# Feed-forward output projections as eight Strassen groups and three plain groups

## The chip, the cores and the metric

The kernel runs on one core of one Trainium2 chip. The metric is the device time of one execution in microseconds. PE is the matrix engine (TensorE), DVE the vector engine, ACT the scalar engine, POOL GpSimd, SP the engine that issues most transfers.

## The reference, cut to what matters

Two transformer blocks work on 512 rows of 1024 numbers in float32. Between them they hold three feed-forwards of the same sizes (1024 to twice 2816, and 2816 back to 1024), each followed by a norm:

```python
def _conv_ffn(x, w_in, conv_w, conv_b, w_out):        # twice, in the first block
    u = x @ w_in
    u = sum(conv_w[j] * up[:, j:j + s] for j in range(CONV_WIDTH)) + conv_b
    g, val = u[..., :D_FF], u[..., D_FF:]
    return (jax.nn.silu(g) * val) @ w_out
...
x = _layer_norm(DN_ALPHA * x + f, ln_ffn_g[layer], ln_ffn_b[layer])
...
gate, up = jnp.split(h2 @ w_gate_up[i], 2, axis=-1)   # once, in the second block
ffn = (jax.nn.silu(gate) * up) @ w_down[i]
x = x + rms_norm(ffn, norm2_post[i])
```

## The kernel before, in words

Every number is carried as a high and a low part in the engine's reduced float32 format, and a product takes three matmuls: high by high, high by low, low by high. `split` (L189) makes the parts: ACT copies the high part, DVE subtracts it to get the low part. `wchunk` (L172) loads 1024 columns of weights into one of three raw buffers and splits them into one of four `whi`/`wlo` buffers.

The 2816 inner columns are worked in 11 groups of 256. For a group, `w_in(g)` loads four weight chunks (two of the gate, two of the value), and `ws_pairs` (L221) runs 96 matmuls of 512 columns into PSUM: gate and value of the first 128 columns, then of the second 128, 24 matmuls each. They use a pool of three PSUM banks named `mm`; a second pool of four is named `at`. The weight buffers of a group come free one by one in its second half, when the next group's chunks are split into them.

In the first two feed-forwards (`ffn`, L829, called `ffn0` and `ffn1` below) each PSUM bank then passes a convolution of three taps (L836 on ACT, L838 twice on DVE), the gate a Silu (L843), and the product of gate and value (L845) is split into `hh`/`hl`. After six groups the output projection of the first 11 blocks of 128 runs (`out_proj`, L610, through `xs`, L240), after the other five that of the last 11. A block of 128 costs 24 matmuls of 512 columns: four row tiles, two column halves, three matmuls (L257 to L259). The result is added to `self.x` by `res_epi` (L383) with the residual scaled by ALPHA in the first half. In the last half `xs` holds back the last four chunks (`stagger=4`), so that each row tile ends by itself and its layer norm and its transposes (`need`, `later`) run beside the matmuls of the next tile; the last column half sits in the `mm` banks.

In the third feed-forward (`ffn2`, L1486) the output projection of ten of the groups goes by Strassen's scheme in Winograd's form, two groups to a phase (`st_phase`, L1422). `st_operands` (L1392) makes seven 256-wide blocks of a group's inner columns with four DVE sums, and splits them. A phase forms four sums of weight blocks on DVE (L1457 to L1462), splits seven weight blocks, and runs seven products of 12 matmuls (L1439 to L1441). Each product fills two PSUM banks, which ACT copies (first phase) or DVE adds (L1447) into one of seven accumulators. In the last phase the accumulators are summed between the products (L1453). Group 11 is plain, with both column halves of a row tile in one go (`xsn`, L626, matmuls L637 to L639), and the RMS norm of each row tile follows it (L1523 to L1532); the residual tile `x2` is loaded from memory on ACT's queue into one of two buffers.

The order on each engine is made by a scheduler at build time that moves independent instructions past each other; each engine then runs its list in order.

Of the kernel before, what the change touches and what calls it, by code (L numbers as in the profile page):

```python
# [15 lines left out]
S = 512  # L16
D = 1024
# [63 lines left out]
class K:  # L81
# [747 lines left out]
    def ffn(self, l, pool, post, hook):  # L829
        nc, I = self.nc, self.I  # L830
        W1, W2 = I["ffn_w_in"][l], I["ffn_w_out"][l]
        hT = {}
# [8 lines left out]
        def pair(m, gp, vp):  # L841
            g = conv(gp, m)
            nc.scalar.activation(g, g, AF.Silu)  # L843
            v = conv(vp, KF + m)
            nc.vector.tensor_tensor(out=v, in0=g, in1=v, op=ALU.mult)  # L845
            hT[m] = (pool.tile([P, S], F32R, tag="hh", name="hh", bufs=12), pool.tile([P, S], F32R, tag="hl", name="hl", bufs=12))
            self.split(v, *hT[m])

        def w_in(g):
            gc = self.ws_load(W1, g * 256)  # L850
            vc = self.ws_load(W1, DFF + g * 256)
            for mm_, gp, vp in self.ws_pairs(gc, vc, g == 0):
                pair(g * 2 + mm_, gp, vp)

        def w_out(k0, kt, last):
            self.out_proj(W2, k0, kt, lambda k: hT[k0 + k][0], lambda k: hT[k0 + k][1], 1.0 if last else ALPHA, post if last else None)

        for g in range(6):
            w_in(g)
            if g == 1:  # L860
                hook()
        w_out(0, 11, False)
        for g in range(6, 11):
            w_in(g)
        w_out(11, 11, True)
# [555 lines left out]

    def st_phase(self, pool, B, hs, Q, first, bufs, last=False):  # L1422

# [4 lines left out]
        b11, b12, b21, b22 = B[0, 0], B[0, 1], B[1, 0], B[1, 1]  # L1428

        def product(i, block, raw, bank):  # L1430
            w = self.wsplit(raw)
            ps = [bank(), bank()]
            for p in range(2):
                h, l = hs[p]
                for t in range(2):
                    a = h[:, block * 256 + t * P:block * 256 + (t + 1) * P]
                    b = l[:, block * 256 + t * P:block * 256 + (t + 1) * P]
                    wh, wl = (x[:, p * 512:(p + 1) * 512] for x in w)
# [3 lines left out]
            for t in range(2):  # L1442
                q = Q[i][:, t * 512:(t + 1) * 512]
                if first:
                    nc.scalar.activation(q, ps[t], AF.Copy)
                else:
                    V(out=q, in0=ps[t], in1=q, op=ALU.add)  # L1447

        def sum_(a, b, op=ALU.add):
            if last:  # L1450
                for t in range(2):
                    s = slice(t * 512, (t + 1) * 512)
                    V(out=Q[a][:, s], in0=Q[a][:, s], in1=Q[b][:, s], op=op)  # L1453

        t2 = pool.tile([P, 1024], F32, tag="wr", name="wr", bufs=bufs)
        product(0, 0, b11, self.psa)
# [3 lines left out]
        product(6, 5, b12, self.psa)  # L1460
        product(5, 4, t2, self.psum)
        V(out=t2, in0=t2, in1=b21, op=ALU.subtract)  # L1462
        sum_(5, 0)
        sum_(6, 5)
        product(1, 1, b21, self.psa)
        sum_(0, 1)
        product(4, 3, b11, self.psa)
        sum_(5, 4)
        sum_(4, 6)
        sum_(6, 3, ALU.subtract)  # L1470
        product(2, 6, b22, self.psum)
        sum_(5, 2)
        if last:
            Q[3] = Q[6]
            V = lambda out, in0, in1, op: nc.vector.tensor_tensor(out=out, in0=in1, in1=in0, op=ALU.subtract)
        product(3, 2, t2, self.psa)
# [9 lines left out]
    def ffn2(self, pool):  # L1486
# [3 lines left out]
        acc = pool.tile([P, 7, D], F32, name="acc")  # L1490
        Q = {i: acc[:, i, :] for i in range(7)}
        xd = self.xd.rearrange("(t p) d -> t p d", p=P)
        hs, B = {}, {}
        WR = 6

        def w_in(g):
# [7 lines left out]
            if g < 10:  # L1504
                return lambda: hs.setdefault(g, self.st_operands(pool, R))
            else:
                hs[g] = [pool.tile([P, self.BLOCKS], F32R, tag=n, name=n, bufs=3)[:, :1024] for n in ("hh", "hl")]
                self.split(R[:, :1024], *hs[g])

        sst = [self.sm.tile([P, 2], F32, tag="ss3", name="ss3") for _ in range(NT)]  # L1510

        def blk(t, c):
            return Q[((0, 5), (6, 4))[t // 2][c]][:, t % 2 * 512:(t % 2 + 1) * 512]

        def last(c):
            sl = slice(c * 512, (c + 1) * 512)

            def epi(t, ps):
                if c == 0:
                    xt[t] = pool.tile([P, D], F32, tag="x2", name="x2", bufs=2)  # L1520
                    nc.scalar.dma_start(xt[t], xd[t])
                a = blk(t, c)
# [4 lines left out]
                if c == 1:  # L1527
                    r = self.rstd2(sst[t])
                    for i in range(2):
                        s = slice(i * 512, (i + 1) * 512)  # L1530
                        nc.vector.scalar_tensor_tensor(out=xt[t][:, s], in0=blk(t, i), scalar=r, in1=xt[t][:, s], op0=ALU.mult, op1=ALU.add)
# [3 lines left out]
        xt = {}  # L1535
        w_in(0)()
        w_in(1)()
        for g in range(0, 10, 2):
            B = self.st_load(pool, W2, g, WR)
            rest = w_in(g + 2)  # L1540
            self.st_phase(pool, B, (hs[g], hs[g + 1]), Q, g == 0, WR, g == 8)
            if g < 8:
                rest()
                w_in(g + 3)()
        h, l = hs[10]
        self.xsn([(W2, c * 512, last(c)) for c in range(2)], 2, lambda k: h[:, k * 512:(k + 1) * 512], lambda k: l[:, k * 512:(k + 1) * 512], 20)

    def run(self):
# [4 lines left out]
        with tc.tile_pool(name="xp", bufs=1) as xp:  # L1553
# [8 lines left out]
            with tc.tile_pool(name="ffn0", bufs=1) as pool:  # L1562
                G, B = self.bcast(I["ln_ffn_g"][0], "G", pool), self.bcast(I["ln_ffn_b"][0], "B", pool)
                dpool = tc.tile_pool(name="diffc", bufs=1, side="right")
                dp = dpool.__enter__()
                self.ffn(0, pool, self.norm_post(G, B, pool.tile([P, S], F32, name="jk")), lambda: self.load1(dp))
# [3 lines left out]
            with tc.tile_pool(name="ffn1", bufs=1) as pool:  # L1570
                G, B = self.bcast(I["ln_ffn_g"][1], "G", pool), self.bcast(I["ln_ffn_b"][1], "B", pool)
                G1 = self.bcast(I["norm1_pre_2"][0], "G1", pool)
# [3 lines left out]
                jk = pool.tile([P, S], F32, name="jk")  # L1576

                def post(t):
                    self.layer_norm(t, G, B, jk)
                    nc.gpsimd.dma_start(xd[t], self.x[:, t, :])  # L1580
                    h = pool.tile([P, D], F32, tag="hn", name="hn", bufs=4)
                    ss = self.sm.tile([P, 2], F32, tag="ss4", name="ss4")
                    for i in range(2):
                        hs = slice(i * 512, (i + 1) * 512)
                        nc.scalar.activation(jk, self.x[:, t, hs], AF.Square, scale=1.0 / 32, accum_out=ss[:, i:i + 1])
                    r = self.rstd2(ss)
                    for i in range(2):
                        hs = slice(i * 512, (i + 1) * 512)
                        nc.vector.scalar_tensor_tensor(out=h[:, hs], in0=self.x[:, t, hs], scalar=r, in1=G1[:, hs], op0=ALU.mult, op1=ALU.mult)
                    self.later(t, lambda: self.to_T(h, t))  # L1590
                self.ffn(1, pool, post, lambda: self.load2(self.kp))
# [30 lines left out]
```

## Time and profile before

| | |
|---|---|
| median of 3 runs | 2115.29 us (2115.05 to 2115.59) |
| the profiled execution | 2115.29 us, its span 2113.1 us |
| PE busy in the span | 2057.3 us (97%) |
| DVE busy | 1416.6 us (67%) |
| ACT busy | 1045.1 us (49%) |
| mean granted PE clock | 0.995 |

The span is the time from the first to the last instruction, so about 2 us of the execution lie outside it. Busy is the union of an engine's instructions; a matmul's own duration overlaps the next one's, so its cost is read from the distance of two starts. In the rows, `A<-B` is what an instruction writes and reads, and the part in brackets or after the last bar is how long the engine sat idle before it and what released it.

### The profile page before, as it was taken

To read this page: it belongs to the slowest core of one execution; us is meant where nothing else is said; L and a number is where in the kernel's file an instruction comes from. 1 tells how busy PE (TensorE), PEld (TensorE's weight loads), DVE (VectorE), ACT (ScalarE), POOL (GpSimd) and SP (SyncE) were. 2 spreads that over 40 slices of the span, in tenths; PEclk is the share of its full clock that TensorE was granted. 3 is DMA by queue.
4 is the path that set the end of the run, shared out by engine and by line. 5 is a ranking of instruction groups with operands and counts; after the bars stand their busy time and mean duration, and the time that the engine had idled before them with its cause. 6 is when DMAs were issued, how large, how long until landed. Compare 5 with 4: busy or idle time off the path is not lost.

```text
span 2113.1 us, 28021 instructions
## 1 busy us (share of the span) xinstructions
PE 2057.3 (97%) x10647; PEld 1739.4 (82%) x10647; DVE 1416.6 (67%) x2608; ACT 1045.1 (49%) x1874; POOL 72.8 (3%) x109
## 2 busy tenths in 40 slices
PE   8999999999999999999999998999999999999996
PEld 7888888888888788888888887877898878888885
DVE  5777876535636788775536547897798555576558
ACT  4777554324425977444324434666475344433332
POOL 0000000000000000110000001000000010000000
PEclk9999999999999999999999999999999999999998
DMA  6221233232323221152323333211323426232321
GB/s 168 61 61 60 71 118 116 89 104 80 106 84 100 60 70 55 57 162 89 105 85 109 96 95 102 70 31 35 105 61 90 150 91 201 81 117 90 104 75 60
DMA packets 197533, 193.71 MB, mean 92 GB/s; under 512 B 8998, under 2 KB 170519, under 8 KB 197399
## 3 DMA queue, kind: packets, MB, share of 16 engines
q1 hardware_dynamic: 191462, 173.04, 27.0%
q0 software_dynamic: 4928, 15.22, 2.4%
q10 hardware_dynamic: 1008, 3.67, 0.5%
q8 instruction: 84, 1.38, 0.3%
q14 instruction: 51, 0.41, 0.1%
HBM read 185.61 MB, written 6.29 MB: 91 GB/s over the span
## 4 chain that ended last, share of the span: by engine, by line
PE 49%; DVE 4%; ACT 1%; issue 1%; POOL 1%; DMA 0%; DVEq 0%; POOLq 0%; ACTq 0%
PE mm L217 10%; PE mm L218 10%; PE mm L219 10%; PE at L258 1%; PE at L259 1%; PE at L257 1%; PE mm L258 1%; PE mm L259 1%; PE mm L257 1%; PE at L1440 1%; PE at L1441 1%; PE at L1439 1%; PE mm L292 1%; PE mm L293 1%; PE mm L291 1%
## 5 line engine op out<-in xcount | busy, mean ns | idle before, releaser
L217 PE MATMUL mm<-xTh,whi 128*128 128x512 f32 (+1 forms) x1584 | 605.2, 382 | 1.6 <-DVE Pt L465 1.3
L219 PE MATMUL mm<-xTh,wlo 128*128 128x512 f32 (+1 forms) x1584 | 604.3, 382 | 0.1
L218 PE MATMUL mm<-xTl,whi 128*128 128x512 f32 (+1 forms) x1584 | 604.2, 382 | 0.0
L186 DVE TENSOR_TENSOR wlo<-raw,whi 128x1024 fp32r<-128x1024 f32 (+3 forms) x314 | 372.6, 1189 | 255.8 <-ACT whi L185 252.1
L185 ACT ACTIVATE whi<-raw 128x1024 fp32r<-128x1024 f32 (+3 forms) x314 | 323.7, 1035 | 415.1 <-PE mm L218 191.4
L217 PEld LDWEIGHTS mm<-xTh,whi 128*128 128x128 f32 x1584 | 298.4, 188 | 56.4 <-issue 1.7
L219 PEld LDWEIGHTS mm<-xTh,wlo 128*128 128x128 f32 x1584 | 298.4, 188 | 55.6 <-DVE wlo L186 0.3
L218 PEld LDWEIGHTS mm<-xTl,whi 128*128 128x128 f32 x1584 | 298.8, 189 | 54.7 <-DVE xTl L194 0.2
L838 DVE SCALAR_TENSOR_TENSOR cy<-mm,cols,cy 128x511 f32<-128x511 f32 (+1 forms) x172 | 128.6, 748 | 107.4 <-ACT cy L836 104.5
L292 PE MATMUL mm<-wlo,xTh 128*128 128x256 f32 x416 | 117.8, 284 | 0.8 <-DVE wlo L186 0.8
L291 PE MATMUL mm<-whi,xTh 128*128 128x256 f32 x416 | 118.1, 285 | 0.3 <-ACT xTh L193 0.2
L293 PE MATMUL mm<-whi,xTl 128*128 128x256 f32 x416 | 117.5, 283 | 0.2 <-DVE xTl L194 0.2
L836 ACT ACTIVATE cy<-mm,cols 128x512 f32<-128x512 f32 x86 | 66.2, 770 | 72.6 <-PE mm L219 72.6
L193 ACT ACTIVATE ph<-at 128x512 fp32r<-128x512 f32 (+3 forms) x128 | 58.6, 474 | 55.1 <-PE at L401 41.4
L258 PE MATMUL at<-wlo,hh 128*128 128x512 f32 x220 | 85.7, 389 | 0.0
L257 PE MATMUL at<-whi,hh 128*128 128x512 f32 x220 | 85.7, 389 | 0.0
L259 PE MATMUL at<-whi,hl 128*128 128x512 f32 x220 | 85.6, 389 | 0.0
L292 PEld LDWEIGHTS mm<-wlo,xTh 128*128 128x128 f32 x416 | 79.5, 191 | 1.9 <-DVE wlo L186 1.0
L291 PEld LDWEIGHTS mm<-whi,xTh 128*128 128x128 f32 x416 | 79.3, 191 | 1.6 <-ACT xTh L193 0.8
L293 PEld LDWEIGHTS mm<-whi,xTl 128*128 128x128 f32 x416 | 79.4, 191 | 1.1 <-DVE xTl L194 0.6
L194 DVE TENSOR_TENSOR pl<-at,ph 128x512 fp32r<-128x512 f32 (+3 forms) x128 | 67.4, 536 | 13.6 <-ACT ph L193 12.6
L401 PE MATMUL at<-ident,Pt 128*128 128x128 f32 x368 | 64.3, 278 | 3.6 <-DVE Pt L784 2.0
(449 smaller groups left out, 3695.9 us busy)
## 6 DMA issues: line engine op xcount, KB each, us to landing
raw<-in_ffn_w_in_dram SPq DMA_DIRECT2D x88, 512.0 KB
raw<-in_w_gate_up_dram SPq DMA_DIRECT2D x44, 512.0 KB
raw<-in_ffn_w_out_dram SPq DMA_DIRECT2D x40, 512.0 KB
raw<-in_w_in_dram SPq DMA_DIRECT2D x40, 512.0 KB
raw<-in_a_w_in_dram SPq DMA_DIRECT2D x22, 512.0 KB
wr<-in_w_down_dram SPq DMA_DIRECT2D x20, 512.0 KB
raw<-in_kv_w_dram SPq DMA_DIRECT2D x16, 512.0 KB
raw<-in_a_w_out_dram SPq DMA_DIRECT2D x8, 512.0 KB
```

The costliest lines, as they stand in the source:

```text
L185: nc.scalar.activation(hi, raw, AF.Copy)
L186: nc.vector.tensor_tensor(out=lo, in0=raw, in1=hi.bitcast(F32), op=ALU.subtract)
L217: mm(o, wh, a, start=(k == 0), stop=False)
L218: mm(o, wh, b, start=False, stop=False)
L219: mm(o, wl, a, start=False, stop=(k == ktiles - 1))
L257: mm(o, a, hi[:, kk, :], start=(k == 0), stop=False)
L258: mm(o, a, lo[:, kk, :], start=False, stop=False)
L259: mm(o, b, hi[:, kk, :], start=False, stop=(k == ktiles - 1))
L291: mm(o, a, hi[:, kk, :], start=(k == 0 and t % 2 == 0), stop=False)
L292: mm(o, a, lo[:, kk, :], start=False, stop=False)
L293: mm(o, b, hi[:, kk, :], start=False, stop=(k == ktiles - 1 and t % 2 == 1))
L838: nc.vector.scalar_tensor_tensor(out=y[:, o:], in0=ps[:, :S - o], scalar=self.c1(f"cw{l}{j}", m), in1=y[:, o:], op0=ALU.mult, op1=ALU.add)
```

## The change

All three feed-forwards now run the same output projection, `st_out`: eight groups by Strassen in four phases, three groups plain. A phase adds three of its products straight to the blocks of the output (`x`, or `acc` in the third feed-forward) and four into accumulators `Q`; `st_final` sums these once, with seven or eight adds of 1024 columns, beside group 9's work. In `ffn0` and `ffn1` the residual is scaled by ALPHA on ACT after group 0. The tile `R` of a group's inner columns has one buffer (two before), the weight blocks `wr` five (six before in `ffn2`), the convolution's `cy` four in `ffn0` and three in `ffn1`. The norm's gain and bias are loaded late into `wr` buffers. In the last plain part all three chunks of the second column half are held back, and that half sits in the four `at` banks, which the transposes use too. In `ffn2` the residual tile is loaded on POOL's queue, when a row tile's second half is done.

```diff
-    def ffn(self, l, pool, post, hook):
+    def ffn(self, l, pool, make_post, hook):
-            y = pool.tile([P, S], F32, tag="cy", name="cy", bufs=4)
+            y = pool.tile([P, S], F32, tag="cy", name="cy", bufs=4 - l)
...
-        w_out(0, 11, False)
-        for g in range(6, 11):
-            w_in(g)
-        w_out(11, 11, True)
+            R = pool.tile([P, 2048], F32, tag="R", name="R", bufs=1)
+            for i, gp, vp in self.ws_pairs(gc, vc, g == 0):
+                y = conv(gp, 2 * g + i)
+                nc.scalar.activation(y, y, AF.Silu)
+                v = conv(vp, KF + 2 * g + i)
+                nc.vector.tensor_tensor(out=R[:, i * 512:(i + 1) * 512], in0=y, in1=v, op=ALU.mult)
+            if g == 0:
+                for t in range(NT):
+                    nc.scalar.activation(self.x[:, t, :], self.x[:, t, :], AF.Copy, scale=ALPHA)
...
+        self.st_out(pool, W2, self.x, False, w_in, last)
...
-    def st_phase(self, pool, B, hs, Q, first, bufs, last=False):
+    def st_phase(self, pool, B, hs, Q, x, first, fresh, bufs):
...
+                if new:
+                    nc.scalar.activation(out(t), ps[t], AF.Copy, scale=1.0 if op == ALU.add else -1.0)
                 else:
-                    V(out=q, in0=ps[t], in1=q, op=ALU.add)
+                    V(out=out(t), in0=out(t), in1=ps[t], op=op)
...
+        product(q(0), first, 0, b11, self.psa)
...
+        product(q(1), first, 5, b12, self.psa)
+        product(q(2), first, 4, t2, self.psum)
...
+        product(xb(0, 0), fresh, 1, b21, self.psa)
+        product(q(3), first, 3, b11, self.psa)
+        product(xb(0, 1), fresh, 6, b22, self.psum)
+        product(xb(1, 0), fresh, 2, t2, self.psa, ALU.subtract)
+
+    def st_final(self, Q, x, fresh):
+        add = lambda out, a, b: self.nc.vector.tensor_tensor(out=out, in0=a, in1=b, op=ALU.add)
...
+    def st_out(self, pool, W, x, fresh, w_in, last, WR=5):
...
+        for g in range(2):
+            group(g, w_in(g))
+        for g in range(0, 8, 2):
+            B = self.st_load(pool, W, g, WR)
+            R = w_in(g + 2)
+            self.st_phase(pool, B, (hs[g], hs[g + 1]), Q, x, g == 0, fresh and g == 0, WR)
+            group(g + 2, R)
+            R = w_in(g + 3)
+            if g == 6:
+                self.st_final(Q, x, fresh)
+            group(g + 3, R)
+        group(10, w_in(10))
+        op = lambda i: lambda k: hs[8 + k // 2][i][:, k % 2 * 512:(k % 2 + 1) * 512]
+        epis = last()
+        for c in range(2):
+            self.xs(W, c * 512, 512, 6, op(0), op(1), epis(c), k0=16, stagger=3 * c, banks=3 * (1 - c))
...
     def ffn2(self, pool):
-        for g in range(0, 10, 2):
-            B = self.st_load(pool, W2, g, WR)
-            rest = w_in(g + 2)
-            self.st_phase(pool, B, (hs[g], hs[g + 1]), Q, g == 0, WR, g == 8)
-            if g < 8:
-                rest()
-                w_in(g + 3)()
-        h, l = hs[10]
-        self.xsn([(W2, c * 512, last(c)) for c in range(2)], 2, lambda k: h[:, k * 512:(k + 1) * 512], lambda k: l[:, k * 512:(k + 1) * 512], 20)
+        self.st_out(pool, W2, acc, True, w_in, lambda: last)
...
-                if c == 0:
-                    xt[t] = pool.tile([P, D], F32, tag="x2", name="x2", bufs=2)
-                    nc.scalar.dma_start(xt[t], xd[t])
...
                 if c == 1:
+                    xt[t] = pool.tile([P, D], F32, tag="x2", name="x2", bufs=2)
+                    nc.gpsimd.dma_start(xt[t], xd[t])
                     r = self.rstd2(sst[t])
```

## Rows read from the trace of the kernel before

**Rows 1.** The page: busy time by engine, and PE's granted clock in 40 slices.

```profile
PE 2057.3 (97%) x10647; PEld 1739.4 (82%) x10647; DVE 1416.6 (67%) x2608; ACT 1045.1 (49%) x1874; POOL 72.8 (3%) x109
...
PEclk9999999999999999999999999999999999999998
```

**Rows 2.** Waits of PE: waiter, releaser, us in total, times, longest.

```profile
PE at L330 <- DMA x<-in_x_dram: 8.9, 1, 8.9
PE mm L1440 <- DVE wlo L194: 5.0, 1, 5.0
```

**Rows 3.** Timeline of PE (start, us), first matmuls of a phase and after it.

```profile
1937.24 0.39 PE L1439 MATMUL at<-whi,hh 128*128 128x512 f32 x1
...
1956.28 0.39 PE L217 MATMUL mm<-xTh,whi 128*128 128x512 f32 x1
```

**Rows 4.** Instructions that read tile `hh`, one of three lines each.

```profile
L257 PE MATMUL at<-whi,hh x220: 389/389/473, 408.5 to 1264.0; 128*128 128x512 f32 x110
L257 PE MATMUL mm<-whi,hh x132: 389/389/478, 438.4 to 1259.3; 128*128 128x512 f32 x132
...
L1439 PE MATMUL at<-whi,hh x100: 389/389/395, 1812.1 to 2088.9; 128*128 128x512 f32 x100
L1439 PE MATMUL mm<-whi,hh x40: 389/389/628, 1817.6 to 2085.5; 128*128 128x512 f32 x40
```

**Rows 5.** Groups of PE instructions by form, the last, plain group of `ffn2`.

```profile
L637 PE MATMUL mm<-whi,hh 128*128 128x512 f32 x16 | 6.3, 396 | 0.1
```

**Rows 6.** Windows: us, busy of PE, PEld, DVE, ACT, POOL; clock, DMA.

```profile
1915.48:1978.04 62.56, 62.56 (x277) 51.80 (x276) 40.86 (x49) 22.03 (x23) 0.00 (x0) 1.00 0.31 101
...
2082.30:2088.40 6.10, 6.10 (x15) 4.80 (x16) 5.47 (x7) 0.00 (x0) 0.00 (x0) 0.53 0.00 0
...
2101.00:2113.10 12.10, 0.00 (x0) 0.00 (x0) 6.78 (x13) 2.17 (x6) 1.41 (x2) 0.67 0.58 203
```

**Rows 7.** Groups of DVE and ACT instructions by form, whole run: count, busy, mean.

```profile
L838 DVE SCALAR_TENSOR_TENSOR cy<-mm,cols,cy 128x511 f32<-128x511 f32 x86 | 64.2, 746 | 104.5 <-ACT cy L836 104.5
L194 DVE TENSOR_TENSOR wlo<-wr,whi 128x1024 fp32r<-128x1024 f32 x35 | 42.4, 1223 | 11.9 <-ACT whi L193 11.6
...
L1447 DVE TENSOR_TENSOR acc<-at,acc 128x512 f32<-128x512 f32 x38 | 24.4, 682 | 0.0
...
L185 ACT ACTIVATE whi<-raw 128x1024 fp32r<-128x1024 f32 x292 | 308.6, 1060 | 375.3 <-PE mm L218 190.0 <-PE at L259 123.6 <-PE at L1441 18.0
```

**Rows 8.** Timeline of DVE over a phase of `ffn2`; gapless between first and last row.

```profile
1930.21 1.23 DVE L194 TENSOR_TENSOR wlo<-wr,whi 128x1024 fp32r<-128x1024 f32 x1 [1.97 <-ACT whi L193]
...
1954.48 1.75 DVE L194 TENSOR_TENSOR hl<-R,hh 128x1536 fp32r<-128x1536 f32 x1
...
1957.35 2.35 DVE L186 TENSOR_TENSOR wlo<-raw,whi 128x1024 fp32r<-128x1024 f32 x2
```

**Rows 9.** Timeline of DVE in the last phase of `ffn2`.

```profile
2077.42 3.69 DVE L1453 TENSOR_TENSOR acc<-acc 128x512 f32<-128x512 f32 x6
2081.03 1.22 DVE L194 TENSOR_TENSOR wlo<-wr,whi 128x1024 fp32r<-128x1024 f32 x1
```

**Rows 10.** Timeline of PE in the last phase of `ffn2`.

```profile
2082.30 0.79 PE L1440 MATMUL mm<-wlo,hh 128*128 128x512 f32 x1 [5.05 <-DVE wlo L194]
2082.90 0.63 PE L1441 MATMUL mm<-whi,hl 128*128 128x512 f32 x1
2083.32 0.63 PE L1440 MATMUL mm<-wlo,hh 128*128 128x512 f32 x1
```

**Rows 11.** The chain that ended last, near the end: start, us, what.

```profile
2100.64 3.76 DMA out_dram<-x
...
2104.48 3.27 DMA x<-xd
```

**Rows 12.** Timeline of DVE, the last row tile's result.

```profile
2107.88 1.41 DVE L1531 SCALAR_TENSOR_TENSOR x<-acc,ss,x 128x512 f32<-128x512 f32 x2 [1.07 <-DMA x<-xd]
```

**Rows 13.** PE in the stage after `ffn1`, behind the norm of its rows.

```profile
1290.12 1.99 PE L953 MATMUL at<-ident,L 128*128 128x128 f32 x8 [2.57 <-ACT L L926]
```

More of the change, by code (lines that the diff above doesn't have):

```diff
@@ L851, in w_in, with last @@
             vc = self.ws_load(W1, DFF + g * 256)
[L852 to L858, printed above, removed]
-            w_in(g)
+            R = pool.tile([P, 2048], F32, tag="R", name="R", bufs=1)
[7 more added lines that the diff above has]
+                    nc.scalar.activation(self.x[:, t, :], self.x[:, t, :], AF.Copy, scale=ALPHA)
             if g == 1:
                 hook()
-        w_out(0, 11, False)
-        for g in range(6, 11):
-            w_in(g)
-        w_out(11, 11, True)
+            return R
+        def last():
+            post = make_post()
+            self.sums = [self.sm.tile([P, 3], F32, tag="sums", name="sums") for _ in range(NT)]
+            self.ns = 2
+            return lambda c: self.res_epi(c * 512, 512, 1.0, c, post if c else None)
+        self.st_out(pool, W2, self.x, False, w_in, last)
     def unit(self, dt=F32):
@@ L1428, in st_phase, with product @@
         b11, b12, b21, b22 = B[0, 0], B[0, 1], B[1, 0], B[1, 1]
-        def product(i, block, raw, bank):
+        q = lambda i: lambda t: Q[i][:, t, :]
+        xb = lambda i, j: lambda t: x[:, 2 * i + t, j * 512:(j + 1) * 512]
+        def product(out, new, block, raw, bank, op=ALU.add):
             w = self.wsplit(raw)
@@ L1472, in st_phase @@
[L1472 to L1476, printed above, removed]
+        product(xb(0, 0), fresh, 1, b21, self.psa)
[4 more added lines that the diff above has]
+        add = lambda out, a, b: self.nc.vector.tensor_tensor(out=out, in0=a, in1=b, op=ALU.add)
+        xb = lambda i, j: x[:, 2 * i:2 * i + 2, j * 512:(j + 1) * 512]
+        p1, p7, p6, p5 = Q
+        add(p6, p6, p1)
+        add(xb(0, 0), xb(0, 0), p1)
+        add(xb(0, 1), xb(0, 1), p6)
+        add(p7, p7, p6)
+        add(xb(0, 1), xb(0, 1), p5)
+        add(xb(1, 0), xb(1, 0), p7)
+        if fresh:
+            add(xb(1, 1), p7, p5)
+        else:
+            add(p7, p7, p5)
+            add(xb(1, 1), xb(1, 1), p7)
@@ new lines, in st_out, with group @@
+    def st_out(self, pool, W, x, fresh, w_in, last, WR=5):
+        hs = {}
+        Q = [pool.tile([P, 2, 512], F32, tag="Q", name="Q", bufs=4) for _ in range(4)]
+        def group(g, R):
+            if g < 8:
+                hs[g] = self.st_operands(pool, R)
+            else:
+                hs[g] = [pool.tile([P, self.BLOCKS], F32R, tag=n, name=n, bufs=3)[:, :1024] for n in ("hh", "hl")]
+                self.split(R[:, :1024], *hs[g])
+        for g in range(2):
[14 more added lines that the diff above has]
+            self.xs(W, c * 512, 512, 6, op(0), op(1), epis(c), k0=16, stagger=3 * c, banks=3 * (1 - c))
@@ L1489, in ffn2 @@
         G = self.bcast(I["norm2_post_2"][0], "G", pool)
-        acc = pool.tile([P, 7, D], F32, name="acc")
-        Q = {i: acc[:, i, :] for i in range(7)}
+        acc = pool.tile([P, NT, D], F32, name="acc")
         xd = self.xd.rearrange("(t p) d -> t p d", p=P)
-        hs, B = {}, {}
-        WR = 6
         def w_in(g):
```

87 lines of the change are left out of this document (27 added, 60 removed).

## The prediction, made before the changed kernel ran

> **What bounds the kernel now.** The page's busy times come first: PE is busy for 2057.3 of 2113.1 us, DVE for 67%, ACT for 49%, and PE's clock stands at its full level in nearly every slice [rows 1]. A busy share alone could hide slow work, so the timeline of PE is next: from the first matmul of a Strassen phase to the first one after it are 19.04 us [rows 3], and a phase holds 84 matmuls, so one of 512 columns costs 0.2267 us and there is no gap between them. Third, PE's waits: its longest wait on another engine is one of 5.05 us on DVE, at the end of `ffn2` [rows 2, 10]. The only longer one, on the input's transfer, is at the start and is not touched. So PE bounds the stages that change, and matmuls taken away there shorten the time one for one, as long as DVE, which must do more, stays behind PE.
>
> **Matmuls.** The rows of `hh` give the projections: (220 + 132) x 3 = 1056 for `ffn0` and `ffn1`, 528 each, and (100 + 40) x 3 = 420 in the five phases of `ffn2` [rows 4], with 16 x 3 = 48 for its plain group [rows 5]. After: four phases of 84 and three groups of 48 are 480 in each. That is 48 fewer in `ffn0`, 48 fewer in `ffn1`, 12 more in `ffn2`: 84 fewer, times 0.2267, **-19.0 us**. `ffn2` alone loses 2.7 us of this.
>
> **The last phase of `ffn2`.** Today its sums of accumulators stand among the products, and six adds in one run of 3.69 us stand ahead of a low half that PE needs [rows 9]. PE idles for 5.05 us and then runs at the low one of its two clock levels: 0.42 us from start to start [rows 10], granted clock 0.53 over the next 6.10 us, in which 15 matmuls run [rows 6]. At full clock these cost 3.4 us, so 2.7 are lost. In the change no phase holds such sums; they are eight adds beside group 9's `w_in`, with group 10's behind them, and no matmul waits for them before the plain part. I take both back: 5.2 (the wait with its release) + 2.7 = **-7.9 us**; the other end is that the wait only moves, 0.
>
> **DVE in `ffn0` and `ffn1`: no wait is shown there today, so this cost is unknown.** What the phases would add is bounded from `ffn2`, which runs them already. One period of `ffn2` (two `w_in` groups and a phase) is 62.56 us, with PE busy throughout and DVE for 40.86 [rows 6]. The convolution adds 16 passes of 0.75 us [rows 7], 12.0 us, to the same period: 52.9 of 62.56 us, 85%. On average there is room. The tight place is the phase itself. DVE works without a gap from 1930.21, the first low half of the phase, until the two low halves of the next group's third and fourth chunks are done, at 1957.35 + 2.35 = 1959.70 [rows 8]. PE starts that group at 1956.28 [rows 3] and wants the third chunk 24 matmuls later, at 1961.7, the fourth at 1964.4. They are there at about 1958.5 and 1959.7: 3.2 and 4.7 us to spare. In `ffn0` and `ffn1` the last gate and the last value of the group before fall into this stretch with four more passes, 3.0 us. That leaves 0.2 and 1.7 us, and about 3 us of operand work (one split of 1.75 [rows 8], three small sums) that could be put behind. So the wait is near 0 by this count but without reserve: I take 0.5 us for each of the eight phases, **+4 us**; the ends are 0, and 2 us a phase, 16 in all. A gain is excluded, since PE loses nothing there now. `st_final` adds eight passes of 1.22 us, by the row of the 1024-column split [rows 7], in the last period only: about 62.7 us of DVE's time, less 2.5 because groups 8 and 9 need no operand sums, against 62.56. What is late then slides into group 10, which has no phase. The seven extra splits and the first phase's copies cost ACT time, too; ACT is busy for 22.03 of 62.56 us [rows 6], so they are hidden, as are the four scalings by ALPHA, near 1.06 us each [rows 7], whose first reader is the first phase's fourth product, two groups later. If ACT's list put them ahead of a weight split, up to 1 us would show.
>
> **Buffers and queues.** With one `R`, group g+3's first write waits for g+2's operand split, done at 1954.48 + 1.75 [rows 8]; in `ffn2` that write is due when the group's first 24 matmuls end, near 1961.7: nothing. With five `wr` a phase's blocks must be read before the next one's load; SP's queue has these loads ahead of the next group's chunks, but a full group (21.8 us) lies between: nothing. The late gain and bias loads stand on POOL's queue, with wr buffers that are free two groups earlier: nothing, and if they were late by a transfer like the 512 KB one of 3.27 us [rows 11], the norm would wait that long.
>
> **The norm behind `ffn1`.** After it PE already waits for the normalised rows (2.57 us at one place [rows 13]), so that stage hangs on DVE and ACT. The norm's work stays, but each row tile now has 18 matmuls for cover where it had 21: three times 0.68 us less, 2.0 us. The fourth tile of the last half also needs an `at` bank that transposes use. In `ffn0` I see no such wait. I take **+2.5 us** for both; ends 0 and 7, the upper one with one more wait like the 2.57.
>
> **The tail of `ffn2`.** No matmul runs in the last 12.1 us [rows 6]. In them the last tile's load waits for an earlier tile's write of 3.76 us on ACT's queue, then takes 3.27 [rows 11], and DVE waits 1.07 us for it [rows 12]. After, a tile has 18 matmuls instead of 12, 4.1 us instead of 2.7, so DVE carries no arrears into the end; but the load still needs the buffer of two tiles before, and POOL, whose queue it joins, must also make the norm's root behind it. Tile 1's write is issued some 4 us after its matmuls (an estimate: three passes near 0.7 us and the pair of 1.41 [rows 12]) and ends 3.8 later, about when tile 3's matmuls end; then a load of 3.3 with its issue, the pair, and a write of 3.8: 9.5 to 10 us. **-2 us**, ends -4.5 (load never late) and +1.
>
> **Sum.** -19.0 - 7.9 + 4 + 2.5 - 2 = -22.4. The profiled execution took 2115.29 us, which is also the median of the three, so this goes against either: **2092.9 us**.
>
> **The rivals.**
> *DVE takes part of it.* In the phases of `ffn0` and `ffn1` the in-order list puts operand work ahead of the next group's low halves; PE waits about 2 us in each: 12 more than forecast, 2105. For it: the 0.2 us left above. Against it: `ffn2` runs the same phases with no wait.
> *DVE takes all of it: slower.* If each of the eight phases ends as the last one does today, 5.2 us idle and 2.7 us of slow clock, that is 63 us in place of 4: 2152. It turns slower than before where a phase costs over 26.4 / 8 = 3.3 us. For it: it has happened once [rows 9, 10]. Against it: that phase carried 14 more adds.
> *The clock falls in the phases.* Around each product PE changes its PSUM banks; were there short gaps at each change and the clock low, 84 matmuls at 0.42 would cost 16 us more per phase, in the eight new ones 130: about 2220. Against it: PE is busy for all of 62.56 us at clock 1.00 in a period with a phase [rows 6]. The Trainium skill, TensorE: Matmul & The Clock Gate, section "A second HAM failure mode: psum-queue depth-cycling", tells of such gaps between groups of matmuls at bank changes, which cost clock though each matmul looks fast; by that rule this rival would be the result, and the trace does not agree for the phases of `ffn2`.
> *`ffn2` gives nothing back.* The wait of the last phase moves to the plain part and the tail stays: 2103.
>
> **How the numbers follow.** Forecast 0.60; part taken by DVE 0.22; `ffn2` gives nothing 0.08; near no change, by both of these together, 0.03; slower by DVE 0.06, by the clock 0.01. What a measurement can tell from no change is about 0.2%, 4.2 us. Of the part taken by DVE 0.02 reach into that band; so faster 0.88, same 0.05, slower 0.07. The forecast's own range is 2086 (no wait in the phases, tail at its better end) to 2099; to hold 8 in 10 it takes in the rivals at 2103 and 2105: 2086 to 2106.
>
> **What the profile after would show.** the phases' lines with 336 matmuls in each feed-forward, and 144 plain ones; PE's busy time down by about 22; no wait of 5 us before the end, and the clock's slices full up to the last; DVE busy near 53 of 62.6 us in a period of `ffn0`. Wrong would be waits of PE on a low half or on a PSUM bank in `ffn0` or `ffn1` that sum to over 12 us, or a granted clock under 1 there; or a tail over 12 us.

## The result and the profile after

The changed kernel takes 2103.52 us (median of four runs, 2102.72 to 2104.43) against 2115.17 of the kernel before beside it: ratio 0.9945, 95% interval 0.993 to 0.996. That is 11.7 us faster, where 22.4 were forecast; the time lies inside the range, near its upper end, and outside the 2086 to 2099 that the forecast gave itself before the rivals at 2103 and 2105 were taken in. The profiled execution took 2104.43 us with a span of 2102.6.

The page of the profile after, busy times and PE's granted clock by slice (answers to [rows 1]):

```profile
PE 2045.3 (97%) x10563; PEld 1729.3 (82%) x10563; DVE 1556.9 (74%) x2776; ACT 1085.2 (52%) x1905; POOL 77.5 (4%) x113
...
PEclk9999999999999999999999999999999999999999
```

PE has 84 matmuls fewer, as counted, and the slice of low clock at the end is gone. But PE's busy time fell by 12.0 us only, not 22 (matmuls at a low clock count as busy for longer). Where the rest went is read from four instructions that stand at the same place of both programs, and the last matmul. Timeline of PE, kernel before:

```profile
659.13 1.04 PE L330 MATMUL at<-ident,x 128*128 128x128 f32 x8
...
908.82 0.28 PE L219 MATMUL mm<-xTh,wlo 128*128 128x256 f32 x1
...
1287.27 0.28 PE L293 MATMUL mm<-whi,xTl 128*128 128x256 f32 x1
...
1726.58 0.39 PE L259 MATMUL mm<-whi,L 128*128 128x512 f32 x1
...
2100.39 0.40 PE L639 MATMUL mm<-whi,hl 128*128 128x512 f32 x1
```

The same places, kernel after:

```profile
653.64 1.03 PE L330 MATMUL at<-ident,x 128*128 128x128 f32 x8
...
902.57 0.28 PE L219 MATMUL mm<-xTh,wlo 128*128 128x256 f32 x1
...
1283.05 0.28 PE L293 MATMUL mm<-whi,xTl 128*128 128x256 f32 x1
...
1723.67 0.39 PE L259 MATMUL mm<-whi,L 128*128 128x512 f32 x1
...
2091.85 0.39 PE L259 MATMUL at<-whi,hl 128*128 128x512 f32 x1
```

After minus before is -5.5, -6.3, -4.2, -2.9 and -8.5 us. The stages between the feed-forwards, which the change doesn't touch, differ by 0.8 us less and 1.3 more; so much two executions differ by. `ffn0` with the joint behind it gave 5.5 at most, `ffn1` (second mark to third) lost 2.0, and `ffn2` (fourth to fifth) gave 5.6. The span shrank by 10.5, so the tail gave 2.0. So `ffn2` and its tail are as forecast, and the first two, which should give 10.9 each by their matmuls, did not.

Where these lose it stands in PE's waits (waiter, releaser, us in total, times, longest; [rows 2] before):

```profile
PE at L330 <- DVE x L381: 5.9, 10, 1.7
PE at L330 <- DVE Q L1600: 5.4, 2, 5.1
PE mm L217 <- ACT whi L185: 3.3, 2, 2.0
...
PE mm L219 <- DVE wlo L186: 2.6, 2, 1.5
```

and in the timeline of PE, the rows that wait:

```profile
300.19 0.50 PE L217 MATMUL mm<-xTh,whi 128*128 128x512 f32 x1 [1.28 <-ACT whi L185]
301.95 0.79 PE L219 MATMUL mm<-xTh,wlo 128*128 128x512 f32 x1 [1.02 <-DVE wlo L186]
...
623.25 1.32 PE L330 MATMUL at<-ident,x 128*128 128x128 f32 x8 [1.67 <-DVE x L381]
...
921.32 0.50 PE L217 MATMUL mm<-xTh,whi 128*128 128x512 f32 x1 [1.99 <-ACT whi L185]
923.60 0.79 PE L219 MATMUL mm<-xTh,wlo 128*128 128x512 f32 x1 [1.54 <-DVE wlo L186]
...
1249.77 1.97 PE L330 MATMUL at<-ident,Q 128*128 128x128 f32 x8 [5.12 <-DVE Q L1600]
```

Two places in each of the two feed-forwards: **between group 0 and group 1** (300 and 921 us), and **the joint**, where the output projection ends and the normalised rows are transposed (623 and 1250 us). None lies in a phase. The groups of PE instructions by form show that, idle time before them in the last column:

```profile
L1440 PE MATMUL at<-whi,hl 128*128 128x512 f32 x240 | 93.4, 389 | 0.0
...
L1440 PE MATMUL mm<-whi,hl 128*128 128x512 f32 x96 | 37.3, 389 | 0.0
```

240 + 96 = 336 for this one of a product's three lines: 28 in each of four phases of three feed-forwards, with no idle time before any. Windows of the changed kernel (columns as in [rows 6]): the first and the second period of `ffn0`, each from the first matmul of a phase to the first of the next; from the last matmul of group 0 to the first of the first phase in `ffn0` and in `ffn1`; the joint behind `ffn1` once PE has stopped waiting; the last 14 us of PE's work; the tail:

```profile
346.58:409.13 62.55, 62.55 (x277) 51.82 (x276) 47.37 (x58) 31.71 (x40) 0.00 (x0) 1.00 0.33 102
409.13:471.69 62.56, 62.56 (x277) 51.82 (x276) 52.20 (x66) 27.51 (x32) 0.00 (x0) 1.00 0.33 101
298.64:346.58 47.94, 45.64 (x196) 37.20 (x194) 39.94 (x52) 24.79 (x31) 0.00 (x0) 0.96 0.29 88
919.06:969.62 50.56, 47.03 (x195) 38.19 (x194) 41.03 (x59) 25.59 (x32) 0.00 (x0) 0.93 0.27 84
...
1249.70:1256.00 6.30, 6.23 (x23) 5.39 (x24) 5.08 (x10) 2.66 (x7) 1.69 (x3) 0.67 0.13 51
2078.00:2091.85 13.85, 13.85 (x62) 11.45 (x61) 7.35 (x15) 2.17 (x6) 2.21 (x4) 1.00 0.32 106
2092.30:2102.60 10.30, 0.00 (x0) 0.00 (x0) 3.72 (x7) 0.72 (x2) 1.13 (x2) 0.73 0.45 154
```

The joint behind `ffn1` costs twice: 5.1 us idle, then a granted clock of 0.67.

### The profile page after: what moved, and what is told of

Read it like the earlier page. It is cut to its first block, busy times and chain, and to the rows that moved or that the text cites. A ratio compares the mean times of both kernels' runs of the same rounds, so it can differ in the third digit from the quotient of the medians.

```text
span 2102.6 us, 28049 instructions
## 1 busy us (share of the span) xinstructions
PE 2045.3 (97%) x10563; PEld 1729.3 (82%) x10563; DVE 1556.9 (74%) x2776; ACT 1085.2 (52%) x1905; POOL 77.5 (4%) x113
## 4 chain that ended last, share of the span: by engine, by line
PE 80%; DVE 7%; ACT 7%; issue 3%; POOL 2%; DMA 2%; POOLq 0%; DVEq 0%; SPq 0%; ACTq 0%
PE mm L219 15%; PE mm L217 15%; PE mm L218 15%; PE at L1439 3%; PE at L1440 3%; PE at L1438 3%; PE mm L291 3%; PE mm L293 3%; PE mm L292 3%; PE at L401 2%; ACT sw L699 1%; DVE wlo L186 1%; PE mm L257 1%; PE mm L259 1%; PE mm L258 1%
## 5 line engine op out<-in xcount | busy, mean ns | idle before, releaser
L185 ACT ACTIVATE whi<-raw 128x1024 fp32r<-128x1024 f32 (+3 forms) x282 | 293.0, 1043 | 311.0 <-PE mm L218 172.7
L186 DVE TENSOR_TENSOR wlo<-raw,whi 128x1024 fp32r<-128x1024 f32 (+3 forms) x282 | 337.2, 1199 | 141.5 <-ACT whi L185 135.6
L193 ACT ACTIVATE whi<-wr 128x1024 fp32r<-128x1024 f32 x84 | 89.0, 1060 | 90.2 <-PE mm L218 29.1
L835 ACT ACTIVATE cy<-mm,cols 128x512 f32<-128x512 f32 x86 | 66.5, 773 | 105.5 <-PE mm L219 105.5
L194 DVE TENSOR_TENSOR wlo<-wr,whi 128x1024 fp32r<-128x1024 f32 x84 | 102.0, 1221 | 12.9 <-ACT whi L193 12.1
L193 ACT ACTIVATE hh<-R 128x256 fp32r<-128x256 f32 (+2 forms) x57 | 54.9, 964 | 82.9 <-DVE R L1528 42.3
L1439 PE MATMUL at<-wlo,hh 128*128 128x512 f32 x240 | 93.4, 389 | 0.0
L1440 PE MATMUL at<-whi,hl 128*128 128x512 f32 x240 | 93.4, 389 | 0.0
L1438 PE MATMUL at<-whi,hh 128*128 128x512 f32 x240 | 92.7, 389 | 0.0
```

Source lines behind the costliest of these rows:

```text
L185: nc.scalar.activation(hi, raw, AF.Copy)
L186: nc.vector.tensor_tensor(out=lo, in0=raw, in1=hi.bitcast(F32), op=ALU.subtract)
L193: nc.scalar.activation(hi, src, AF.Copy)
L1438: mm(ps[t], a, wh, start=p == 0, stop=False)
L1439: mm(ps[t], a, wl, start=False, stop=False)
L1440: mm(ps[t], b, wh, start=False, stop=p == 1)
```

## The experiments

Line numbers in the diffs' text are those of the changed kernel. Each ratio is against the kernel before on the same chip. The runs stand on several chips, so a difference between two variants is taken between their gains over the kernel before beside each; the gain of the changed kernel is 11.7 us.

**e1_banks, e2_loads, e3_noalpha, e4_both: what costs time at the two places.** In the joint the transposes share the `at` banks with the second column half. Between groups 0 and 1, ACT's list has changed. Timeline of ACT after; the Exp of `al` (`load2`) and of `ls` (`load1`), two small constants that a later stage needs, now stand ahead of group 0's first convolution (L835). `al` waits for its transfer, `ls` for a product on DVE that waits for the transfer of `lam` (the last row, of DVE):

```profile
294.09 0.20 ACT L663 ACTIVATE ls<-ls 128x2 f32<-128x2 f32 x1 [7.98 <-issue]
294.20 0.76 ACT L835 ACTIVATE cy<-mm,cols 128x512 f32<-128x512 f32 x1
...
914.68 0.23 ACT L1041 ACTIVATE al<-al 128x32 f32<-128x32 f32 x1 [8.14 <-DMA al<-in_a_log_b_dram]
914.81 0.76 ACT L835 ACTIVATE cy<-mm,cols 128x512 f32<-128x512 f32 x1
...
293.39 0.29 DVE L661 TENSOR_TENSOR lam<-lam 128x128 f32<-128x128 f32 x1 [7.50 <-DMA lam<-in_b_lambda_dram]
```

In the kernel before both stand behind the first convolution. Timeline of ACT before, `ffn1`:

```profile
917.03 0.78 ACT L836 ACTIVATE cy<-mm,cols 128x512 f32<-128x512 f32 x1 [5.20 <-PE mm L219]
...
919.47 0.23 ACT L1044 ACTIVATE al<-al 128x32 f32<-128x32 f32 x1 [1.66 <-DMA al<-in_a_log_b_dram]
```

There the convolution waited 5.2 us for its PSUM bank. In the changed kernel it starts 9.2 us after the end of the same copy of transposed rows on ACT (9.0 in `ffn0`), in place of 5.2, so about 4 us of ACT's 8 are lost; the rest it would have waited for PE. The DMA issues of the changed kernel in this stretch say how late such a small transfer is (KB, median us from issue to landing):

```profile
al<-in_a_log_b_dram POOLq DMA_DIRECT2D x1, 8.0 KB, 8.1
```

The edits, e4 has the first two together:

```diff
# e1_banks
-            self.xs(W, c * 512, 512, 6, op(0), op(1), epis(c), k0=16, stagger=3 * c, banks=3 * (1 - c))
+            self.xs(W, c * 512, 512, 6, op(0), op(1), epis(c), k0=16, stagger=3 * c, banks=3 * (1 - c) if fresh else 3 * c)
# e2_loads, at the start of ffn
+        for n, i in (("ln_ffn_g", l), ("ln_ffn_b", l), ("norm1_pre_2", 0))[:2 + l]:
+            self.bcast(I[n][i], "wr", pool, bufs=5)
# e3_noalpha
-            if g == 0:
-                for t in range(NT):
-                    nc.scalar.activation(self.x[:, t, :], self.x[:, t, :], AF.Copy, scale=ALPHA)
```

> The changed kernel with one edit: in the first two feed-forwards the second column half of the last plain part goes back to the three mm banks, so that the transposes have the four at banks to themselves. Shared-bank theory: the 5.1 us that PE idles behind ffn1 (eight transposes waiting for Q from DVE) and the low clock of the 6 us after it go, the 1.7 us behind ffn0 shrinks; 2103.5 - 6 to 8 = about 2096.5 us. Rival, the cover theory (18 matmuls per row tile in place of 21 are too few, whichever banks they use): the wait moves by 2 us at most, 2101.5 to 2103.5 us.

> The changed kernel with two 512 KB broadcast loads (ffn0) and three (ffn1) put back at the head of POOL's queue at the start of the feed-forward; what they load is never read. List theory: without the early gain and bias loads the scheduler puts small ACT and DVE instructions, which wait 7 to 10 us for the transfers of later constants, ahead of group 0's convolution; with the loads back they stand behind it, PE's waits between group 0 and group 1 (1.3 + 1.0 us in ffn0, 2.0 + 1.5 us in ffn1) and the low clock behind them go: 2103.5 - 5 to 7 = about 2097.5 us. Rival, the ALPHA theory (four scalings of 1.05 us on ACT delay group 1's weight splits): no change, 2103.5, or slower for the extra transfers.

> The changed kernel without the four scalings of the residual by ALPHA in the first two feed-forwards; nothing else is left out. ALPHA theory: eight passes of 1.05 us leave ACT's list in the time before group 1, its weight splits come about 4 us earlier, and PE's waits between group 0 and group 1 go: 2103.5 - 5 to 7 = about 2097.5 us. List theory: the scalings run while ACT is idle and wait for nothing, so their absence changes nothing: 2103.5 within 1 us, with the same four waits.

> Both edits, the mm banks for the second column half and the early loads. If the two causes are separate places in PE's time, their gains add: 2103.5 - 11 to 15 = about 2090.5 us, with no wait of PE over 1.5 us left between the input and the end except the known one for the normalised rows. If one of them only stood in for the other, it is no better than the better of the two alone, about 2097.

Measured: e1 2101.69 us, ratio 0.9941 (0.9928 to 0.9953); e2 2099.47, 0.9931 (0.9919 to 0.9944); e3 2103.99, 0.9951 (0.9938 to 0.9965); e4 2096.89, 0.9919 (0.9905 to 0.9932).

The ALPHA theory falls: without the scalings the time and the waits stay (1.14 and 1.02 us in `ffn0`, 1.90 and 1.86 in `ffn1`). e1 missed: at most 2 us came, which is what its rival, the cover theory, had said. Timeline of PE in e1, the joint behind `ffn1`:

```profile
1249.96 1.32 PE L330 MATMUL at<-ident,Q 128*128 128x128 f32 x8 [1.04 <-DVE Q L1600]
...
1256.81 1.69 PE L330 MATMUL at<-ident,Q 128*128 128x128 f32 x8 [2.86 <-DVE Q L1600]
1258.15 0.78 PE L257 MATMUL at<-whi,hh 128*128 128x512 f32 x1
```

The first tile's transposes wait 1.0 us in place of 5.1, but now the second tile's do, and the last tile's 18 matmuls, ready long since, stand behind them (from 1258.15). So the banks are not the point; the order is. e2 met its mark in `ffn0` only: the two waits there shrank to 0.33 and 0.43 us, while in `ffn1` ACT still sat 7.04 us ahead of the Exp of `al`, whose transfer now lands behind three more of 512 KB, and PE waited 3.10 (its second wait there was 1.03). The gains of e1 and e2 add up in e4 within the intervals, at half of what I had expected.

**e10_depth, e14_depth_only: the order of the joint.** e10 has the edits of e4 and the line below; e14 has that line alone.

```diff
         epis = last()
+        self.depth = 1 if fresh else 2
         for c in range(2):
```

> Bank and load edits as in the run before, and the transposes of row tile t are allocated two tiles later in place of one, so that the last row tile's 18 matmuls stand in PE's list ahead of the second tile's transposes. Order theory (the joint loses time because matmuls that could run stand behind transposes that wait for the norm on DVE): the 2.87 us wait behind ffn1, the 1.0 us one behind ffn0 and the low clock after the first go, 4 to 5 us under the run with both edits: about 2092.5 us. Rival, the chain theory (DVE needs some 7 us for each tile's two norms, more than PE's 18 matmuls of 4.1 us, in whatever order): the wait only moves to the next transposes, no gain over 1 us: about 2096.5.

> The changed kernel with the transposes allocated two row tiles later, and nothing else; the second column half stays in the at banks that the transposes use. Order theory: it was not the shared banks but PE's list that cost time, so the 5.1 us wait behind ffn1 falls to about 1, the 1.7 us behind ffn0 goes, and with the clock 6 to 7 us come back: about 2097 us. Bank theory: as long as the banks are shared the wait stays over 4 us, and the kernel within 2 us of 2103.5.

Measured: e10 2092.51 us, ratio 0.9891 (0.9875 to 0.9906); e14 2094.86, 0.9907 (0.9893 to 0.9922). With one line, e14 stands 19.3 us under the kernel before where the changed one stood 11.7: it gets 7.6 us back, with the shared banks untouched. The traces agree: from the first matmul of the last phase to the last matmul of 256 columns behind the joint are 122.98 us in place of 126.66 in `ffn0`, and 133.47 in place of 137.60 in `ffn1`, 7.8 us less in all. Timeline of PE in e14, the same joint:

```profile
1246.33 1.32 PE L330 MATMUL at<-ident,Q 128*128 128x128 f32 x8 [1.05 <-DVE Q L1601]
...
1254.50 0.66 PE L330 MATMUL at<-ident,Q 128*128 128x128 f32 x4
```

Three tiles' matmuls run ahead of the first transposes, the fourth's behind them, and the second tile's transposes wait for nothing. The bank theory, the chain theory and e1's cover theory fall: each row tile has 18 matmuls as in the changed kernel, and in this order they are cover enough. After this idle time of 1.05 us, PE's clock stays at 1.00 (window of e14 behind it):

```profile
1246.33:1251.60 5.27, 5.26 (x26) 4.30 (x27) 5.14 (x12) 3.72 (x6) 1.13 (x2) 1.00 0.00 0
```

**e6_third_only, e7_dve_half: the terms that the forecast got right, and DVE's reserve.** e6 is the kernel before with the change in `ffn2` alone. e7 adds in `product`, L1430:

```diff
             w = self.wsplit(raw)
+            if x is self.x:
+                V(out=w[1][:, :512], in0=raw[:, :512], in1=w[0].bitcast(F32)[:, :512], op=ALU.subtract)
```

> The kernel before in the first two feed-forwards, the change in the third alone. By the terms of the prediction: 12 more matmuls + 2.7, the last phase - 7.9, the tail - 2 = - 7.2 us against the kernel before, about 2107 us; the rival that ffn2 gives nothing back says + 1 to + 3, about 2116.

> The changed kernel with seven more DVE passes of 0.68 us (512 columns of each product's low half computed a second time, the same values) in each of the eight phases of ffn0 and ffn1, 4.8 us a phase. Reserve theory (the changed kernel runs its phases with 1 to 2 us to spare at the next group's third and fourth low halves and some 3 us of operand work that can wait): PE begins to wait in the phases, 1 to 3 us in each with its low clock, 8 to 30 us in all, 2112 to 2134 us. Rival (DVE has ample room, the count of the prediction was far too careful): no wait over 0.5 us in a phase, 2103.5 within 2.

Measured: e6 2107.47 us, ratio 0.9964 (0.9952 to 0.9977), 6.8 us under the kernel before: the terms of `ffn2` and the tail hold, and the rival that `ffn2` gives nothing back falls. e7 2135.0 us, ratio 1.0101 (1.0087 to 1.0115), 20.8 over the kernel before, so 32.4 over the changed one. PE's waits in e7:

```profile
PE mm L217 <- ACT whi L185: 8.3, 10, 2.4
PE at L1441 <- DVE wlo L1432: 7.1, 12, 0.7
...
PE at L1440 <- DVE Q L1447: 4.1, 6, 0.7
```

and two periods of its `ffn0`, the first from the first matmul of a phase to that of the next, the second from one wait of a phase to the same one of the next:

```profile
346.30:409.00 62.70, 62.70 (x277) 51.74 (x276) 51.58 (x65) 31.62 (x39) 0.00 (x0) 1.00 0.32 101
413.94:480.70 66.76, 64.17 (x276) 51.57 (x276) 56.15 (x73) 27.56 (x31) 0.00 (x0) 1.00 0.31 95
```

The second period is 66.76 us where the changed kernel has 62.56: of 4.8 us added to DVE in a phase, 4.2 come out as time, though DVE is busy for only 56 of 67. The first period takes the same 4.8 us at next to no cost (62.70 us): its phase leaves the copies of four products to ACT, and DVE was busy for 47.37 us there, not 52.20. So the later phases of the changed kernel run with well under 1 us to spare, the first one with over 4. I had looked for the waits at the next group's third and fourth low halves; in the phases they come at the low halves of the products themselves, which the added passes write, and at the accumulators, which hold PE's banks. So e7 tests the reserve at the products, and not at the place that the prediction counted.

**e11_al, e12_z, e15_best: the late constants.** e11 takes e10 and ties the Exp of `al` to group 3. e12 drops the extra loads of e2 and ties the product of `lam` (and with it the Exp of `ls`), the Exp of `al` and the cast of `sel` to a zero made from group 1's `R`; e15 ties two gain vectors more. Cut to what matters:

```diff
             if g == 1:
-                hook()
+                z = self.sm.tile([P, 2], F32, tag="nm", name="nm")[:, 0:1]
+                nc.vector.tensor_scalar(out=z, in0=R[:, 512:513], scalar1=0.0, scalar2=None, op0=ALU.mult)
+                hook(z)
...
-        nc.scalar.activation(self.al, self.al, AF.Exp)
+        nc.scalar.activation(self.al, self.al, AF.Exp, bias=z)
...
-        V.tensor_copy(self.sel2, sel)
+        V.scalar_tensor_tensor(out=self.sel2, in0=sel, scalar=z, in1=sel, op0=ALU.add, op1=ALU.max)
# e15, in the tables' load
+            nc.vector.scalar_tensor_tensor(out=g, in0=g, scalar=z, in1=g, op0=ALU.add, op1=ALU.max)
```

> As the run with the depth edit, and the Exp of al on ACT in ffn1 is made to wait for a result of group 3 (its bias is a zero worked out from R), so that it can't stand ahead of group 0's Silu. In the run with both edits ACT still sat 5.2 us before it for a transfer, and PE waited 1.26 + 1.02 + 0.43 us between group 0 and group 1 of ffn1. List theory: these three waits and the low clock behind them go, 3 to 4 us: about 2089 us. Rival (group 1's splits are late for another reason, as ACT's or DVE's own work in group 0): no change, about 2092.5.

> Bank and depth edits; no extra loads; instead every small instruction of the two prefetch routines that reads a late constant (the product of lam, the Exp of ls and of al, the cast of sel) takes a zero worked out from group 1's R as an operand, so that none of them can stand ahead of group 0's convolution on ACT or DVE. List theory: no wait of PE over 0.6 us between group 0 and group 1 in either feed-forward, 4 us under the run with depth, banks and loads: about 2088.5 us. Rival (what is late there is group 1's weight transfers or ACT's own work): no better than that run, 2092.5.

Measured: e11 2092.54 us, ratio 0.9893 (0.9879 to 0.9906), no change from e10; e12 2090.58, 0.989 (0.9873 to 0.9906), 1.8 us better than e10. Both missed in `ffn1`, and the timeline of DVE says why. In e11:

```profile
915.49 0.18 DVE L1052 CAST sel<-c_selssd 128x32 fp32r<-128x32 f32 x1 [7.49 <-DMA c_selssd<-const_selssd_dram]
```

In e12, where that cast is gone from the place:

```profile
912.22 0.42 DVE L883 TENSOR_TENSOR ctq<-c_axcos,gainq 128x256 f32<-128x256 f32 x1 [6.29 <-DMA gainq<-in_q_norm_dram]
```

One consumer taken away, the next one waited in the same place, with a 4.09 us wait of PE behind it. In `ffn0`, e12 has no wait left there. e15 takes the last one away (and has the tail of e13, below).

> As the run before it (banks, depth, zero operand, tail), with the two gain vectors of the attention tables of the second block tied to the zero as well. There they still stood behind their transfers ahead of group 0's second pair of convolution passes in ffn1: DVE sat 6.29 us, and PE 4.09 us at the first low half of group 1. List theory: that wait goes and with it the low clock behind it, 4 to 5 us under the run before it: about 2085.5 us, with no wait of PE over 0.6 us between group 0 and group 1 of either feed-forward. Rival (the next thing in the list, or the weights themselves, is late by as much): no change, about 2090.

Measured: 2083.91 us (2082.49 to 2085.1), ratio 0.9853 (0.9837 to 0.9869): 30.6 us under the kernel before, 19.0 more than the changed one, the fastest here. PE's waits in e15, the longest after the input's:

```profile
PE at L330 <- DVE x L381: 3.3, 7, 0.8
PE at L953 <- ACT L L926: 3.3, 2, 2.4
```

No wait for `whi`, `wlo` or `Q` is among the longest seven; between group 0 and group 1 of both feed-forwards PE waits for nothing. The stretch from the last matmul of group 0 to the first phase is now 43.67 us in both feed-forwards, here in `ffn1`, where the changed kernel took 47.94 and 50.56:

```profile
911.87:955.54 43.67, 43.67 (x196) 36.18 (x194) 38.05 (x62) 23.75 (x30) 0.00 (x0) 1.00 0.31 97
```

That is 4.3 + 6.9 = 11.2 us, waits and low clock together: what the late constants cost the changed kernel.

**e13_best: the tail.** e12, and the residual tiles of `ffn2` go into freed `Q` buffers.

```diff
-                if c == 1:
-                    xt[t] = pool.tile([P, D], F32, tag="x2", name="x2", bufs=2)
+                if c == 0:
+                    xt[t] = pool.tile([P, D], F32, tag="Q", name="Q", bufs=4)
                     nc.gpsimd.dma_start(xt[t], xd[t])
+                if c == 1:
```

> As the run with the zero operand, and ffn2's residual tiles are loaded into the four freed Q buffers when a row tile's first column half is done, so that the last tile's load no longer waits for the write of two tiles before. Tail theory: the 1.67 us wait for the write goes, 1.5 us under that run, about 2087 us. Rival (the tail hangs on DVE and POOL, not on this load): the same as that run.

Measured: 2090.33 us, ratio 0.9887 (0.9873 to 0.9902), 0.25 under e12, where 1.5 was expected. The chain that ended last of the changed kernel has the two transfers ahead of the last result:

```profile
2088.89 4.02 DMA out_dram<-x
2093.46 2.00 DMA x<-xd
```

In e13's chain neither stands; from the first row tile's reduction on ACT to the last result are 15.33 us against 16.95 in e12. The last write, longer by some 0.6 us, gave that much of these 1.6 back, so that from the last matmul to the span's end are 9.8 us in place of 10.7. The median shows only 0.25 of this 1.0; the spread of either kernel is about 2 us, so the size is left open.

## Why the prediction was right, and where not

**The number.** 2103.5 is where two rivals stood: `ffn2` gives nothing back (2103) and DVE takes part in the phases (2105). Neither happened: e6 refutes the first, the phases without idle time the second. The range held only because it had been widened for them, so that part is luck. By the prediction's own signs it was partly wrong: PE's busy time fell by 12.0 us and not 22, a wait of 5.12 us stood before the end, and the granted clock was 0.96 and 0.93 between group 0 and the first phase of `ffn0` and `ffn1`.

**Right: the matmuls.** 84 fewer, 0.2267 us each, no idle time before the 336 matmuls of a line: -19.0 stands, and nothing in the phases takes from it.

**Right: the last phase of `ffn2` and the tail.** `ffn2` gave 5.6 us where +2.7 - 7.9 = -5.2 was forecast, the tail 2.0 where 2 was, and e6 measured the two together at -6.8 against -7.2. The last 14 us run at clock 1.00, where [rows 6] has 0.53. The tail is 10.3 us by the window, a little over the 9.5 to 10 of the working, and held by the write-then-load chain that it named.

**The phases in `ffn0` and `ffn1`: +4 forecast, 0 measured.** The period came out right: 52.20 us of DVE in 62.56, forecast 52.9. The reserve came out small, as counted (0.2): under 1 us by e7, though at the products and not at the next group's low halves, and not in the first phase of a feed-forward. The step that was off is the half microsecond per phase, taken as insurance between two ends; the lower one was true. The rivals in which DVE takes part or all fall, but not by much: with 4.8 us of DVE work more per phase the kernel is slower than before (e7). The rival that the clock falls in the phases falls, too, at a granted clock of 1.00 for 62.56 us of unbroken work. The Trainium skill, TensorE: Matmul & The Clock Gate, section "A second HAM failure mode: psum-queue depth-cycling", describes short idle times of PE between groups of matmuls as PSUM banks are cycled, at which the clock falls again and again; the trace does not show that here (0.0 us idle).

**Wrong: "The late gain and bias loads stand on POOL's queue ...: nothing."** I asked who waits for the moved loads, and not what moves forward when they leave the head of the queue. With them gone, the small consumers (0.2 us each) of the prefetched constants behind them were put ahead of group 0's convolution in the in-order lists of ACT and DVE; their transfers take up to 8.1 us, the weight splits of group 1 wait behind them, and PE behind those. e2 shows in `ffn0` that the order hangs on these loads; that the scheduler expected the constants earlier is inferred. They did not come earlier: the Exp of `al`, which waited for its transfer in both kernels, ran 7.7 us after the end of ACT's copy of transposed rows in the kernel before and 9.1 us after it in the changed one. The windows of the changed kernel and of e15 put the cost at 11.2 us; from e14, which has this cost and not the joint's, to e15 are 11.4 us by the gains, 1.0 of them the tail's by the traces of e12 and e13. My term was 0 with an upper end of a 3.3 us transfer at another place. The Trainium skill, PSUM — Partial Sum Buffer, section "Engine vs sequencer instructions", says that the queues of ScalarE, VectorE and GpSimd are strictly first in, first out; the rows of ACT at 294 and 914 us and of DVE in e11 and e12 agree: a ready convolution sits behind an Exp of 0.2 us for about 4 us.

**Mis-sized: the norm behind `ffn1` (and `ffn0`), +2.5 with ends 0 and 7.** It cost 7.6 to 7.8, by the gains and the traces of e14 and the changed kernel. The working had named the reduced cover (18 matmuls for 21) and a bank that transposes use, and priced them at a third. It had also misread a row: the 2.57 us of [rows 13] is PE waiting for the attention's keys (`L`, L926), later in that stage; the same wait stands in the changed kernel at 2.50 us (the expectation of e4 reads it the same way). For the normalised rows (`hn`) the kernel before waited 0.86 us. Timeline of PE before, then after:

```profile
1257.63 0.66 PE L330 MATMUL at<-ident,hn 128*128 128x128 f32 x4 [0.86 <-DVE hn L1589]
...
1285.83 1.99 PE L950 MATMUL at<-ident,L 128*128 128x128 f32 x8 [2.50 <-ACT L L923]
```

What the working left out is what PE's list does with them: with the column half in the same pool, the first tile's transposes stood ahead of the third tile's 18 matmuls. PE then waited 5.12 us with these 18 behind the wait, which e14 shows to be ready, and lost about 2 us more at a clock of 0.67 for 6.30 us.

The sum by these sizes: -19.0 - 7.9 + 0 + 11.2 + 7.8 - 2 = -9.9, against -10.5 between the two spans that were traced and -11.7 by the medians. With both new waits gone and the tail's load moved, -28.9 - 1.0 = -29.9, against -30.6 in e15. So the terms of the gain were sound, and the shortfall is two new waits in stages whose work had hardly changed. One slip of the description: in `ffn2` `R` keeps two buffers, so the step on its first write was needless.

## What to carry to other kernels

When a change takes a transfer out of a queue, ask what moves forward as well as what moves back: where a scheduler fills the lists of in-order engines, a 0.2 us consumer of a late constant can land ahead of the main work, and taking one away brings up the next, so tie all of them to a result that comes late enough. Where a stage ends tile by tile into a norm, read PE's order, not only the number of matmuls that cover the norm: ready matmuls behind waiting transposes are no cover. And a count that leaves 0.2 us of reserve can be right; test it by adding work at the place that was counted, before more is put on that engine. And follow a wait to its tile before pricing a term by it.

## What was not expected of the hardware

Small broadcasts were slow: the 8 KB of `al` on POOL's queue took 8.1 us from issue to landing, behind other loads of that queue and beside the weight stream, longer than the 512 KB load of [rows 11], 3.27 us; in the kernel before the same 8 KB took 4.9. Why is not shown. And the price of idle time on PE was not even. Two waits between groups 0 and 1 of `ffn0` were followed by 3.42 us at a granted clock of 0.50 in the changed kernel (1.28 and 1.02 us) and by no fall at all in e14 (1.29 and 1.02 us), so half of these 3.42 us, 1.7, is a difference that two executions with the same waits can show. After 1.05 us of idle time at the joint (e14) the clock stayed at 1.00, and after 4.09 us (e12) it was 0.60 over the next 4.31:

```profile
916.69:921.00 4.31, 4.31 (x12) 3.44 (x13) 4.31 (x8) 2.45 (x4) 0.00 (x0) 0.60 0.41 122
```

Those 4.31 us held 12 matmuls, which at 0.2267 us are 2.7 us: 1.6 us lost to the clock behind 4.09 lost to the wait.
